# The output projections of both layers in weight units of 512 columns by 4 blocks, summed four token tiles at a time

## The chip, the cores and the metric

One core of a Trainium2 chip runs the whole program. The metric is the device time of one execution in microseconds (us), as the median of several runs. The engines are called by the profile's names: PE multiplies (PEld is its weight load), DVE is the vector engine, ACT the scalar engine, POOL the general one, SP issues most DMAs. Each engine takes its own instructions strictly in the order that was fixed when the program was built, and semaphores tie the engines together.

## What is computed

One inference step of a two-layer decoder. Layer 0 is a gated linear attention, layer 1 a differential attention; each ends with an output projection, and each is followed by a normalization and an MLP.

```python
def gla_output(o, r, g_norm, w_out, dtype):       # layer 0
    ...
    return o.astype(dtype) @ w_out
def diff_output(o, g_sub, lam_init, w_out, dtype):  # layer 1
    ...
    return o.reshape(B, T, DIFF_HEADS * DIFF_DV).astype(dtype) @ w_out
def post_norm(x, f, g, b):
    return layer_norm(DEEPNORM_ALPHA * x + f, g, b)
```

The 1024 prompt tokens are multiplied in each layer by a weight `w_out` of 1024 x 1024 in fp32. The result is added to the residual (times ALPHA) and normalized; the MLP of that layer reads the normalized rows. Beside this, eight running sequences are attended over 256 pages of keys and 256 pages of values in a cache; that work is spread as background over layer 0's projection, its MLP and layer 1's input projection.

## The kernel before

**The projection.** `w_out(w, scaled, side)` (L1004 to L1030) is called twice: for layer 0 at L1154 (`scaled` False) and for layer 1 at L1492 (`scaled` True). It multiplies 8 tiles of 128 tokens with the weight, whose 1024 rows are 8 blocks k of 128. An fp32 product is made of three matmuls (`mm3`, L205 to L208): the activations are held as a high part XH and a rest XL, the weight as whi and wlo, and XH x whi, XH x wlo and XL x whi are summed in one psum bank. The activations (128 x 128) are the operand that is loaded into PE, the weight's columns stream past.

The weight comes in *units* of 2048 columns in SBUF, each a pair whi, wlo. A unit here (`kunit`, L198) is all 8 blocks by 256 columns. `unit` (L182 to L196) loads it in four chunks of 128 x 512: for each a DMA from SP into a buffer `raw` (two of them, in pool wrp), a cast on ACT to whi (L193), a subtraction on POOL to wlo (L194). A chunk of a `kunit` covers two blocks by 256 columns, in rows of 1 KB.

The pool wsp holds two whi and two wlo, so two units are on chip at a time; the next unit takes the buffer of whichever unit is let go first, and its first cast waits for the last matmul that reads the old one.

**The order.** The four units u are taken with the two token halves c (tiles 0 to 3, tiles 4 to 7) as (0,0) (1,0) (0,1) (1,1) (2,0) (3,0) (2,1) (3,1): (u, c). For each pair there are two accumulations; each fills one psum bank `mmt` with two token tiles of 256 columns (24 matmuls for a tile, 48 for a bank). There are three mmt banks, three axt banks (for transposes, and for some of the MLP's tiles in layer 1) and two smt banks. A full bank is added to the residual Y by one DVE instruction of 128 x 512 (L1022 in layer 1; L1024 in layer 0, with ALPHA). After every odd u the two tiles are handed to `normalize` (L1040), which takes their statistics per 512 columns (L1045), and after the second 512 columns normalizes pairs of tiles (L1049 to L1060); after tile 3 and after tile 7 `to_fm` (L1066) transposes the four tiles through axt banks and makes XH and XL, or in layer 1 XR, for the MLP.

**What sets the order of instructions.** The program is written in the order above, and a planner turns it into the order of each engine when it is built: of what is ready by its own estimate of times, the earliest written goes first. So PE may take matmuls of a later tile while an earlier one waits, as far as psum banks and weights allow. Background work (`background`, L852: the pages) has the lowest priority.

**Around layer 0.** Before it PE ends the gate projection, whose last unit lets its buffer go shortly before `w_out` starts. At the same time SP issues four loads of the residual (1 MB each, L1151) and begins with pages of keys (512 KB each, L880), each multiplied by the query on DVE or POOL (L911) and reduced on DVE (L912). `side` is the generator of pages; `w_out` calls it 12 times. Some pages are tied behind the last step in `steps_v`, the list of DVE steps that the evictions (L1024) are added to. Behind it comes `mlp` (L1097), whose first two units follow in the wsp buffers.

**Around layer 1.** The planner starts `w_out` while the last head of the attention still runs: `o_fm` (L1339) turns the attention's output of one block k and one token half into XH and XL: four transposes on PE (L1343), ACT (L1344), DVE (L1345). Token half 0 is made early, half 1 only after the last head (block by block, k from 0 to 7), so matmuls of half 0 fill PE's gaps in between. The psum pools are opened anew here: the mmt banks lie where the attention's score banks (`prt`) were. The residual comes back from DRAM (L1442). `side` is one step there, the small tokens' normalization. Behind it comes `mlp1` (L1672), whose tiles take axt and mmt in turn, and whose DVE work (L1700, L1560, L203) begins before `w_out` ends.

Of the kernel before, what the change touches and what calls it, by code (L numbers as in the profile page):

```python
# [16 lines left out]
ALU = mybir.AluOpType  # L17
# [4 lines left out]
P = 128  # L22
D = 1024
T = 1024
NB = 8
# [6 lines left out]
ALPHA = 4.0 ** 0.25  # L32
# [82 lines left out]
def hybrid_step(ctx, tc, A, dbg=None, upto=9):  # L115
    nc = tc.nc
    V, S, G, TE = nc.vector, nc.scalar, nc.gpsimd, nc.tensor
# [21 lines left out]
    def pairt():  # L139
        return banks["pr"].tile([P, 2, 512], F32, name="prt")  # L140

    def mmt():
        return banks["mm"].tile([P, 512], F32, name="mmt") if "mm" in banks else pairt()[:, 0]

    def axt():
        return banks["ax"].tile([P, 512], F32, name="axt")
# [22 lines left out]
    def xh_part(c, i):  # L169
        return cp.tile([P, 4, TH], F32R, name="XH%d%d" % (c, i), tag="XH%d%d" % (c, i))  # L170

    XH = Halves([[xh_part(c, i) for i in range(2)] for c in range(2)])
    XL = Halves([cp.tile([P, NB, TH], F32R, name="XL%d" % c, tag="XL%d" % c) for c in range(2)])
    Y = cp.tile([P, 8192], F32, name="Y")
    Yt = Y.rearrange("p (t n) -> p t n", n=D)
# [6 lines left out]
    def unit(n, *srcs):  # L182

        hi = wsp.tile([P, 2048], F32R, name="whi")
        lo = wsp.tile([P, 2048], F32R, name="wlo")
        at = 0
        for src in srcs:
            step = 512 // n
            for x in range(0, src.shape[1], step):
                raw = wrp.tile([P, 512], F32, name="raw")  # L190
                dma(raw.rearrange("p (k n) -> p k n", n=n), src[:, x : x + step, :])
                c = slice(at, at + 512)
                S.copy(hi[:, c], raw)  # L193
                G.tensor_tensor(lo[:, c], raw, hi[:, c].bitcast(F32), op=ALU.subtract)  # L194
                at += 512
        return hi, lo  # L196

    def kunit(w, c0):  # L198
        return unit(256, w.rearrange("(k p) n -> p k n", p=P)[:, :, c0 : c0 + 256])
# [5 lines left out]
    def mm3(ps, ah, al, bh, bl, first, last):  # L205
        TE.matmul(ps, ah, bh, start=first, stop=False)  # L206
        TE.matmul(ps, ah, bl, start=False, stop=False)  # L207
        return TE.matmul(ps, al, bh, start=False, stop=last)  # L208
# [121 lines left out]
    hv, lv = (w.rearrange("p (i k n) -> p i k n", i=2, n=P) for w in qku)  # L330
# [12 lines left out]
    ps = smt()  # L343
# [16 lines left out]
    ps = smt()  # L360
# [156 lines left out]
    parts = []  # L517
# [9 lines left out]
    for k in range(NB):  # L527
        w = sload(wi[k * P : (k + 1) * P, 0:2048])
# [6 lines left out]
    for k in range(0, NB, 2):  # L535
        w = sload2(wi[:, 2048:3072], k)
# [20 lines left out]
    ps = smt()  # L557
# [4 lines left out]
    ps = smt()  # L562
# [3 lines left out]
    pv = ps.rearrange("p (h c t) -> p c h t", h=GH, c=4)  # L566
# [4 lines left out]
    ps = smt()  # L571
# [15 lines left out]
    ps = smt()  # L587
# [5 lines left out]
    for hh in range(2):  # L593
        ps = smt()
# [13 lines left out]
    ps = smt()  # L608
    pv = ps[:TS, :128].rearrange("p (h t) -> p h t", t=TS)
# [3 lines left out]
    for s in (8, 4, 2, 1):  # L613
        u = t2()[:, :128]
        level(sb.rearrange("p h t -> p (h t)"), sqk[:, :128], sqk[:, 128:], u, s, V)
        ps = smt()
        pv = ps[:TS, :128].rearrange("p (h t) -> p h t", t=TS)
# [53 lines left out]
    ps = smt()  # L671
# [125 lines left out]
    for h in range(1, GH):  # L797
# [6 lines left out]
        for c in range(2):  # L804
            parts = decays(h, c, pgs[c])
# [7 lines left out]
    for h in range(GH):  # L813
        hi, lo = kunit(wi, 2048 + h * 256)
        hv, lv = (w.rearrange("p (k n) -> p k n", n=256) for w in (hi, lo))
        silt = st2.rearrange("p k (c n) -> p k c n", c=2)
        for c in range(2):
            cs = slice(512 * c, 512 * c + 512)
            sil, pts = [], []
            for m in range(2):  # L820
                ps = mmt()
# [43 lines left out]
    lv = lpt[:, :256].rearrange("p (i j d) -> p i j d", i=2, j=2)  # L865
# [137 lines left out]

    def w_out(w, scaled, side=None):  # L1004

        units = {}
        n = 0
        for u, c in ((0, 0), (1, 0), (0, 1), (1, 1), (2, 0), (3, 0), (2, 1), (3, 1)):
            if u not in units:
                units[u] = kunit(w, u * 256)  # L1010
            hv, lv = (x.rearrange("p (k n) -> p k n", n=256) for x in units[u])
            for i2 in range(2):
                ps = mmt()
                t0 = 4 * c + 2 * i2
                for i in range(2):
                    a = slice((t0 + i) * P, (t0 + i + 1) * P)
                    for k in range(NB):
                        mm3(ps[:, i * 256 : (i + 1) * 256], XH[:, k, a], XL[:, k, a], hv[:, k, :], lv[:, k, :], k == 0, k == NB - 1)
                yv = Yt[:, t0 : t0 + 2, u * 256 : (u + 1) * 256]
                pv = ps.rearrange("p (i n) -> p i n", n=256)  # L1020
                if scaled:
                    V.tensor_tensor(yv, yv, pv, op=ALU.add)  # L1022
                else:
                    steps_v.append(V.scalar_tensor_tensor(yv, yv, ALPHA, pv, ALU.mult, ALU.add).ins)  # L1024
                if side and (n == 4 if scaled else n < 12):
                    next(side)
                n += 1
                if u % 2:
                    for t in (t0, t0 + 1):
                        yield t, u // 2  # L1030

    def ln_stats(pool):
        st = pool.tile([P, 8, 2, 6], F32, name="bst")
# [4 lines left out]
    steps_v, steps_g = [], []  # L1038
# [162 lines left out]
    units, outs = {}, []  # L1201
    for u, t2_ in ((u, t) for u in range(12) for t in range(4)):
# [5 lines left out]
        hv, lv = units[u]  # L1208
        ps = mmt()
        for i in range(2):  # L1210
            t = 2 * t2_ + i
            a = slice(t * P, (t + 1) * P)
# [6 lines left out]
        if u < 8:  # L1219
            tmp = qt.tile([P, 2, 4, 16], F32, name="qr")  # L1220
            pv = ps.rearrange("p (i n d) -> p i n d", i=2, d=64)
# [129 lines left out]
    ps = smt()  # L1351
# [36 lines left out]
    for step in steps + [None] * 0:  # L1388
        if step:
            h, n, t = step  # L1390
# [19 lines left out]
        if n % 4 == 3:  # L1410
            ts = (slice(0, 4), slice(4, 8))[n // 4] if h == 7 else slice(t % 2, 8, 2)
            S.copy(Yd[:, ts, h], po.rearrange("p (t e) -> p t e", e=P))
            for i in range(4):
                x = po[:, i * P : (i + 1) * P]
# [85 lines left out]
    acc = [smt(), smt()]  # L1500
# [246 lines left out]
```

## Time and profile before

| | us |
|---|---|
| median of 3 runs | 2808.88 (2805.65 to 2810.58) |
| the profiled execution | 2803.96 |
| its span, first to last instruction | 2802.2 |
| mean granted clock of PE | 0.993 |
| layer 0's `w_out`, its first matmul to the first of the MLP | 489.0 to 582.9 |
| layer 1's `w_out`, its first matmul to its last | 2000.3 to 2112.9 |
| evictions L1022 and L1024 | 16 each, 0.69 each |

The span is what the profile shows; the execution's own time has 1.8 us more around it. Matmul rows show a duration that overlaps the next one's, so the price of a matmul is the distance between starts, not the duration. In rows of groups, "idle before" is the idle time of that engine just before the group's instructions, with what ended it.

### The profile page before, as it was taken

To read this page: it belongs to the slowest core of one execution; us is meant where nothing else is said; L and a number is where in the kernel's file an instruction comes from. 1 tells how busy PE (TensorE), PEld (TensorE's weight loads), DVE (VectorE), ACT (ScalarE), POOL (GpSimd) and SP (SyncE) were. 2 spreads that over 40 slices of the span, in tenths; PEclk is the share of its full clock that TensorE was granted. 3 is DMA by queue.
4 is the path that set the end of the run, shared out by engine and by line. 5 is a ranking of instruction groups with operands and counts; after the bars stand their busy time and mean duration, and the time that the engine had idled before them with its cause. 6 is when DMAs were issued, how large, how long until landed. Compare 5 with 4: busy or idle time off the path is not lost.

```text
span 2802.2 us, 52241 instructions
## 1 busy us (share of the span) xinstructions
PE 2715.8 (97%) x19849; PEld 2233.8 (80%) x19849; DVE 1954.0 (70%) x3045; ACT 1096.4 (39%) x2233; POOL 1105.1 (39%) x744
## 2 busy tenths in 40 slices
PE   8988999999999999999999999999999999999997
PEld 5866767987777777777798988776899889797985
DVE  5466463668877777777677730887648888979788
ACT  4324363152231221221241112777535546355553
POOL 2142112243443343433234222100026677687774
PEclk9999999999999999999999999999999999999998
DMA  7565654735889898888658995122144455555584
GB/s 234 168 231 194 215 183 170 267 96 183 311 317 335 307 351 307 315 319 305 235 197 302 363 365 169 55 61 74 37 120 91 102 146 115 141 121 122 132 187 91
DMA packets 275624, 562.81 MB, mean 201 GB/s; under 512 B 23510, under 2 KB 144412, under 8 KB 271276
## 3 DMA queue, kind: packets, MB, share of 16 engines
q1 hardware_dynamic: 256076, 522.75, 54.1%
q0 software_dynamic: 19296, 36.71, 8.1%
q8 instruction: 156, 2.56, 0.4%
q14 instruction: 96, 0.79, 0.1%
HBM read 533.00 MB, written 29.52 MB: 201 GB/s over the span
## 4 chain that ended last, share of the span: by engine, by line
PE 74%; DVE 8%; ACT 4%; DMA 3%; issue 2%; POOL 1%; SPq 0%; DVEq 0%; POOLq 0%; ACTq 0%
PE mmt L206 17%; PE mmt L207 17%; PE mmt L208 17%; PE smt L952 4%; PE axt L206 3%; PE axt L207 3%; PE axt L208 3%; PE smt L1323 2%; ACT as L1301 2%; DVE pg L911 1%; PE prt L1297 1%; DMA swt<-in_mlp_w 1%; PE axt L1318 1%; DMA rw<-in_mlp_w 1%; PE smt L686 1%
## 5 line engine op out<-in xcount | busy, mean ns | idle before, releaser
L194 POOL TENSOR_TENSOR wlo<-raw,whi 128x512 fp32r<-128x512 f32 x252 | 364.4, 1459 | 730.6 <-ACT whi L193 599.6
L206 PE MATMUL mmt<-whi,XH 128*128 128x256 f32 (+1 forms) x1760 | 524.6, 300 | 1.3 <-DVE ast L1299 0.9
L207 PE MATMUL mmt<-wlo,XH 128*128 128x256 f32 (+1 forms) x1760 | 522.2, 298 | 0.4 <-POOL wlo L194 0.4
L206 PE MATMUL mmt<-XH,whi 128*128 128x512 f32 (+1 forms) x1216 | 434.2, 358 | 6.6 <-DVE Y L1022 3.0
L208 PE MATMUL mmt<-XH,wlo 128*128 128x512 f32 (+1 forms) x1216 | 432.0, 356 | 0.0
L208 PE MATMUL mmt<-whi,XL 128*128 128x256 f32 x1536 | 431.7, 284 | 0.0
L193 ACT CAST whi<-raw 128x512 fp32r<-128x512 f32 x252 | 150.5, 620 | 579.3 <-PE mmt L208 189.6
L206 PEld LDWEIGHTS mmt<-whi,XH 128*128 128x128 f32 x1760 | 330.7, 189 | 39.1 <-issue 24.3
L912 DVE TENSOR_REDUCE sc<-pg 128x16 f32<-128x1024 f32 x256 | 308.2, 1211 | 70.5 <-POOL pg L911 68.1
L207 PEld LDWEIGHTS mmt<-wlo,XH 128*128 128x128 f32 x1760 | 332.2, 189 | 17.5 <-issue 6.8
L207 PE MATMUL mmt<-XL,whi 128*128 128x512 f32 x768 | 306.9, 400 | 0.0
L911 DVE TENSOR_TENSOR pg<-pg,qb 128x1024 f32<-128x1024 f32 x192 | 262.7, 1375 | 57.9 <-DMA pg<-in_cache_k 46.8
L208 PEld LDWEIGHTS mmt<-whi,XL 128*128 128x128 f32 x1536 | 288.3, 189 | 4.4 <-issue 3.8
L206 PEld LDWEIGHTS mmt<-XH,whi 128*128 128x128 f32 x1216 | 229.0, 189 | 50.8 <-issue 7.5
L911 POOL TENSOR_TENSOR pg<-pg,qb 128x1024 f32<-128x1024 f32 x64 | 165.4, 2585 | 253.1 <-DMA pg<-in_cache_k 168.4
L208 PEld LDWEIGHTS mmt<-XH,wlo 128*128 128x128 f32 x1216 | 229.4, 189 | 36.4 <-issue 3.7
L206 PE MATMUL mmt<-whi,HH 128*128 128x512 f32 x512 | 204.6, 401 | 4.9 <-DVE Y L1136 3.4
L208 PE MATMUL mmt<-whi,HL 128*128 128x512 f32 x512 | 203.9, 398 | 0.0
L207 PE MATMUL mmt<-wlo,HH 128*128 128x512 f32 x512 | 203.4, 397 | 0.0
L1586 POOL TENSOR_TENSOR wlo<-RW,whi 128x512 fp32r<-128x512 f32 x96 | 166.1, 1767 | 58.1 <-ACT whi L1585 58.0
L1586 POOL TENSOR_TENSOR wlo<-rw,whi 128x512 fp32r<-128x512 f32 x92 | 156.8, 1778 | 79.1 <-ACT whi L1585 78.8
L207 PEld LDWEIGHTS mmt<-XL,whi 128*128 128x128 f32 x768 | 145.2, 189 | 38.4 <-issue 7.2
(438 smaller groups left out, 5707.8 us busy)
## 6 DMA issues: line engine op xcount, KB each, us to landing
pg<-in_cache_k SPq DMA_DIRECT2D x256, 512.0 KB
pg<-in_cache_v SPq DMA_DIRECT2D x256, 512.0 KB
raw<-in_mlp_w SPq DMA_DIRECT2D x164, 256.0 KB
swt<-in_mlp_w SPq DMA_DIRECT2D x32, 1024.0 KB
rw<-in_mlp_w SPq DMA_DIRECT2D x116, 256.0 KB
RW<-in_mlp_w POOLq DMA_DIRECT2D x96, 256.0 KB, 5.8
swt<-in_gla_w_in SPq DMA_DIRECT2D x12, 1024.0 KB
swt<-in_diff_w_in SPq DMA_DIRECT2D x12, 1024.0 KB
```

What stands on the lines that cost most here:

```text
L193: S.copy(hi[:, c], raw)
L194: G.tensor_tensor(lo[:, c], raw, hi[:, c].bitcast(F32), op=ALU.subtract)
L206: TE.matmul(ps, ah, bh, start=first, stop=False)
L207: TE.matmul(ps, ah, bl, start=False, stop=False)
L208: return TE.matmul(ps, al, bh, start=False, stop=last)
L686: TE.matmul(ps[o : o + TS, :], lhs[:, k + 2 * j + i, :], ts[j][:, i, c * 512 : (c + 1) * 512], start=k == 0 and j == 1, stop=k == nk - 4 a ...
L911: eng.tensor_tensor(pg, pg, qb, op=ALU.mult)
L912: return V.tensor_reduce(sc[:, n, :], pg.rearrange("p (h d) -> p h d", d=64), op=ALU.add, axis=AX.X).ins
L952: m = TE.matmul(acc[i * TS : i * TS + 16, :256], w[r, n, :], pg[r, i * 256 : (i + 1) * 256], start=n == 0, stop=n == NPG).ins
L1301: S.activation(sc_[:, m, :W], sc_[:, m, :W], AF.Exp, bias=mns[:, m : m + 1], scale=-1.0, accum_out=l[:, m : m + 1])
L1323: TE.matmul(out, at, v, start=j == 0, stop=j == t + 1)
L1586: G.tensor_tensor(lo[:, k, :], t, hi[:, k, :].bitcast(F32), op=ALU.subtract)
```

## The change

Both calls of `w_out` get another tiling. A unit is now 4 blocks by 512 columns (as in the MLP's second weight, L1129), so the two units of one half u of the columns are its upper and lower 512 rows (kk = 0, 1). Both are asked for at the top of u. For each token half c four accumulations are open at once, one tile of 512 columns each, in three mmt banks and one axt bank. They are first summed over unit kk = c (4 tiles x 4 blocks x 3 matmuls), then over unit 1 - c, and each tile is evicted when its second pass ends: the same 16 evictions of 128 x 512 in each layer. A matmul streams 512 columns instead of 256, so there are 384 in a layer instead of 768. A DMA row is 2 KB instead of 1 KB, a chunk is one block by 512 columns. Half c = 1 begins with unit 1 and ends with unit 0. The pages are called 12 times still, now at every second half of a tile (odd n below 24), before the eviction instead of behind it; layer 1's `side` step comes at n = 9 of 32 instead of n = 4 of 16.

```diff
-        units = {}
         n = 0
-        for u, c in ((0, 0), (1, 0), (0, 1), (1, 1), (2, 0), (3, 0), (2, 1), (3, 1)):
-            if u not in units:
-                units[u] = kunit(w, u * 256)
-            hv, lv = (x.rearrange("p (k n) -> p k n", n=256) for x in units[u])
-            for i2 in range(2):
-                ps = mmt()
-                t0 = 4 * c + 2 * i2
-                for i in range(2):
-                    a = slice((t0 + i) * P, (t0 + i + 1) * P)
-                    for k in range(NB):
-                        mm3(ps[:, i * 256 : (i + 1) * 256], XH[:, k, a], XL[:, k, a], hv[:, k, :], lv[:, k, :], k == 0, k == NB - 1)
...
-                if side and (n == 4 if scaled else n < 12):
-                    next(side)
-                n += 1
-                if u % 2:
-                    for t in (t0, t0 + 1):
-                        yield t, u // 2
+        for u in range(2):
+            parts = [w[512 * kk : 512 * kk + 512, 512 * u : 512 * u + 512].rearrange("(k p) n -> p k n", p=P) for kk in range(2)]
+            halves = [[x.rearrange("p (k n) -> p k n", n=512) for x in unit(512, part)] for part in parts]
+            for c in range(2):
+                acc = [mmt(), mmt(), mmt(), axt()]
+                for kk in (c, 1 - c):
+                    hv, lv = halves[kk]
+                    for i, ps in enumerate(acc):
+                        t = 4 * c + i
+                        a = slice(t * P, (t + 1) * P)
+                        for k in range(4):
+                            x = 4 * kk + k
+                            mm3(ps, XH[:, x, a], XL[:, x, a], hv[:, k, :], lv[:, k, :], kk == c and k == 0, kk != c and k == 3)
+                        if side and (n == 9 if scaled else n % 2 and n < 24):
+                            next(side)
+                        n += 1
+                        if kk == c:
+                            continue
+                        yv = Yt[:, t, 512 * u : 512 * u + 512]
...
+                        yield t, u
```

More of the change, by code (lines that the diff above doesn't have):

```diff
@@ L1004, in w_out @@
     def w_out(w, scaled, side=None):
-        units = {}
         n = 0
-        for u, c in ((0, 0), (1, 0), (0, 1), (1, 1), (2, 0), (3, 0), (2, 1), (3, 1)):
-            if u not in units:
-                units[u] = kunit(w, u * 256)
-            hv, lv = (x.rearrange("p (k n) -> p k n", n=256) for x in units[u])
-            for i2 in range(2):
-                ps = mmt()
-                t0 = 4 * c + 2 * i2
-                for i in range(2):
-                    a = slice((t0 + i) * P, (t0 + i + 1) * P)
-                    for k in range(NB):
-                        mm3(ps[:, i * 256 : (i + 1) * 256], XH[:, k, a], XL[:, k, a], hv[:, k, :], lv[:, k, :], k == 0, k == NB - 1)
[L1019 to L1024, printed above, removed]
-                if side and (n == 4 if scaled else n < 12):
-                    next(side)
-                n += 1
-                if u % 2:
-                    for t in (t0, t0 + 1):
-                        yield t, u // 2
@@ new lines, in w_out @@
+        for u in range(2):
[17 more added lines that the diff above has]
+                        yv = Yt[:, t, 512 * u : 512 * u + 512]
+                        if scaled:
+                            V.tensor_tensor(yv, yv, ps, op=ALU.add)
+                        else:
+                            steps_v.append(V.scalar_tensor_tensor(yv, yv, ALPHA, ps, ALU.mult, ALU.add).ins)
+                        yield t, u
```

## The prediction

> **What bounds the kernel now.** I read the page first: who is busy, and what the chain that ended last consists of.
>
> ```profile
> span 2802.2 us, 52241 instructions
> PE 2715.8 (97%) x19849; PEld 2233.8 (80%) x19849; DVE 1954.0 (70%) x3045; ACT 1096.4 (39%) x2233; POOL 1105.1 (39%) x744
> PE 74%; DVE 8%; ACT 4%; DMA 3%; issue 2%; POOL 1%; SPq 0%; DVEq 0%; POOLq 0%; ACTq 0%
> ```
>
> PE is busy for 97% of the span and is 74% of the chain: a microsecond saved on PE is a microsecond saved at the end, unless something else is late next. So I looked at PE in the two stretches that the change touches, first as busy time by stretch (length, then PE, PEld, DVE, ACT, POOL busy and instructions, granted clock, DMA share, GB/s), then as the list of its waits: around layer 0's stretch one row, around layer 1's the other five.
>
> ```profile
> 489.00:582.90 93.90, 93.90 (x799) 93.90 (x796) 54.35 (x88) 22.88 (x35) 27.76 (x20) 1.00 0.65 218
> 2000.30:2112.90 112.60, 111.71 (x951) 111.09 (x952) 55.27 (x96) 37.91 (x73) 26.22 (x20) 1.00 0.36 104
> PE mmt L206 <- DVE HL L203: 1.5, 1, 1.5
> ...
> PE mmt L206 <- DVE Y L1022: 3.0, 1, 3.0
> PE mmt L206 <- DVE ast L1299: 0.9, 2, 0.6
> ...
> PE axt L1071 <- ACT XR L1077: 0.4, 1, 0.4
> PE mmt L206 <- ACT XH L1344: 0.2, 1, 0.2
> ```
>
> In layer 0 PE does not stop once in 93.9 us, at clock 1.00: 768 matmuls of 256 columns and 32 transposes lie back to back. Its one wait of 1.5 us comes later, in the MLP. In layer 1 it loses 0.9 us inside the stretch and 3.0 us just behind it. All that better ordering could return is therefore 6.0 us (1.5 + 3.0 + 0.9 + 0.4 + 0.2), and only the three last rows and the 3.0 us lie near the projection. The rest of any gain has to come from cheaper matmuls. In a kernel of 2808.88 us, 0.2% is 5.6 us, about what a measurement can tell from no change.
>
> **The change part by part. 1. The matmuls.** 768 matmuls of 256 columns in each layer become 384 of 512, over both layers 768 pairs that each become one. Their price is the distance between starts. I take an undisturbed stretch of layer 1's projection, and one of layer 0's second MLP weight, which already has the new form (4 blocks by 512 columns, weights streaming). L206 is every third matmul.
>
> ```profile
> L206 PE MATMUL mmt<-whi,XH x58: 277/280/283, 2065.7 to 2085.9; 128*128 128x256 f32 x58
> L206 PE MATMUL mmt<-whi,HH x27: 392/397/400, 640.4 to 658.7; 128*128 128x512 f32 x27
> ```
>
> 20.2 us over 57 x 3 steps are 118.1 ns; 18.3 us over 26 x 3 are 234.6 ns. A pair costs 236.2, so merging saves 1.6 ns, and 768 x 1.6 = 1.3 us. The starts are rounded to 0.1 us, which leaves 2.5 ns of doubt in a pair: from 3.2 us gained to 0.6 lost. I take -1.3: the granted clock is 1.00 in both.
>
> The Trainium skill, page "TensorE: Matmul & The Clock Gate", section on why a gap is 56 ns and not 53.3, gives a warm matmul N columns at 2.4 GHz plus a fixed 2.5 ns or so. By that rule each merging would save the whole fixed part, 768 x 2.5 = 1.9 us, and the sum would come out 0.6 us lower. Here the two rows disagree with it in kind: they lie 11 and 21 ns above N / 2.4, so most of the excess grows with the columns and is not saved; the measured 1.6 ns decides.
>
> **2. Evictions and loads.** The 16 evictions of 128 x 512 stay (0.68 us each, first row), and so do the chunks of 256 KB with a cast and a subtraction each. They cost nothing as long as a unit is there when PE wants it. In the rows before, a unit is let go at 523.38 and at 538.87 (ACT's first cast follows at once) and complete when POOL's last row ends, at 533.41 and 547.30:
>
> ```profile
> L1024 DVE SCALAR_TENSOR_TENSOR Y<-Y,mmt 128x512 f32<-128x512 f32 x15 | 10.3, 684 | 23.0 <-PE mmt L208 22.9
> 523.38 1.14 ACT L193 CAST whi<-raw 128x512 fp32r<-128x512 f32 x2 [14.89 <-PE mmt L208]
> 538.87 1.23 ACT L193 CAST whi<-raw 128x512 fp32r<-128x512 f32 x2 [6.82 <-DMA raw<-in_gla_w_out]
> 530.52 2.89 POOL L194 TENSOR_TENSOR wlo<-raw,whi 128x512 fp32r<-128x512 f32 x2 [2.88 <-ACT whi L193]
> 546.01 1.29 POOL L194 TENSOR_TENSOR wlo<-raw,whi 128x512 fp32r<-128x512 f32 x1 [0.25 <-ACT whi L193]
> ```
>
> That is 10.0 and 8.4 us. In the new order half c = 1 reads unit 1 first and unit 0 last; unit 1 is let go one pass early, and a pass over one unit is 4 x 4 x 3 = 48 matmuls x 234.6 ns = 11.3 us. So the next half's first unit has 11.3 us for 10.0, and the second, let go at the turn, again 11.3 for 8.4. Cost 0, covered by that pass, with 1.3 us to spare at the tighter place; a load slower by more than that would show as a stall of the difference.
>
> **3. Layer 0's second unit.** This is the place with the least cover. The unit's last chunk is issued late, behind loads of the residual, and lands late:
>
> ```profile
> 499.09 2.46 SPq L191 DMA_DIRECT2D raw<-in_gla_w_out  x2
> 507.87 0.62 ACT L193 CAST whi<-raw 128x512 fp32r<-128x512 f32 x1 [13.06 <-DMA raw<-in_gla_w_out]
> 508.57 1.29 POOL L194 TENSOR_TENSOR wlo<-raw,whi 128x512 fp32r<-128x512 f32 x1 [14.96 <-ACT whi L193]
> 509.67 0.51 PE L206 MATMUL mmt<-whi,XH 128*128 128x256 f32 x3
> ```
>
> Its whi is ready at 508.49, its wlo at 509.86. Before, PE had 22 us of work on the first unit alone (both token halves), and the last row, three L206 in a row for three open banks, shows it arriving just then without a stop. Now only 11.3 us are on the first unit, and half 1 starts with the late one. But three of its four blocks are there by then: 36 matmuls x 234.6 = 8.4 us. 489.0 + 11.3 + 8.4 = 508.7, and the 8 matmuls that need only the last block's whi last 1.9 us more, to 510.6. If PE goes block by block through its four open banks, nothing is lost; if it goes tile by tile, it stops at 502.4 (three blocks, 9 matmuls, after 500.3) until 509.9, which is 7.5 us. The planner already ordered around this chunk once, so I take nearly the lower end, +0.4, for the banks, which now fill nearly together and wait for DVE behind its pages; ends 0 and 7.5.
>
> **4. Layer 1's start.** PE stops twice while XH, XL and banks arrive.
>
> ```profile
> 2000.30 0.36 PE L206 MATMUL mmt<-whi,XH 128*128 128x256 f32 x1 [0.22 <-DVE ast L1299]
> ...
> 2001.09 0.39 PE L206 MATMUL mmt<-whi,XH 128*128 128x256 f32 x1 [0.19 <-ACT XH L1344]
> ...
> 2002.23 0.39 PE L206 MATMUL mmt<-whi,XH 128*128 128x256 f32 x1 [0.64 <-DVE ast L1299]
> ```
>
> A matmul twice as long fills more of the same gap, but the bank that PE waits for at 2002.23 (a score bank that DVE still reads) comes no sooner. Of 0.8 us (0.19 + 0.64) I take half: -0.4; ends 0 and -0.8.
>
> **5. Layer 1's token half 1.** Until the last head is done PE lives on half 0:
>
> ```profile
> 2000.30:2033.30 33.00, 21.81 (x155) 19.20 (x156) 2.06 (x3) 0.00 (x0) 1.00 0.22 69
> 2033.93 1.61 DVE L1345 SCALAR_TENSOR_TENSOR XL<-axt,gs,XH 128x512 fp32r<-128x512 f32 x2 [3.17 <-ACT XH L1344]
> 2043.06 0.75 DVE L1345 SCALAR_TENSOR_TENSOR XL<-axt,gs,XH 128x512 fp32r<-128x512 f32 x1
> ```
>
> By 2033.30 it had used 156 of the 192 matmuls that units 0 and 1 have for half 0, 18.4 us. The new half 0 holds as much, 96 x 234.6 = 22.5 us, so 4.1 us are left, and the 32 transposes of half 1 go between (0.1 us each: what 768 x 118.1 ns = 90.7 us leaves of layer 0's 93.9 us, over its 32): PE is fed until 2033.3 + 4.1 + 3.2 = 2040.6. Before, half 1 started with block 0, one of the two of the 2033.93 row; now it starts with block 4, which the last row shows ready at 2043.81. Taken as it stands, PE stops for 3.2 us. But DVE made two blocks in 1.61 us when it had them, so with PE free for the transposes block 4 could come at 2033.9 + 5 x 0.8 = 2037.9, before the gap. I take +0.8, nearer to the second, since PE's own filler is what held the blocks up; ends 0 and 3.2.
>
> **6. Layer 1's end.** The 3.0 us wait is for a psum bank:
>
> ```profile
> 2103.36 6.21 DVE L1700 SCALAR_TENSOR_TENSOR Y<-Y,RP 128x1024 f32<-128x1024 f32 x3 [0.48 <-PE axt L1071]
> 2111.72 0.68 DVE L1022 TENSOR_TENSOR Y<-Y,mmt 128x512 f32<-128x512 f32 x1
> 2118.18 0.67 DVE L1022 TENSOR_TENSOR Y<-Y,mmt 128x512 f32<-128x512 f32 x1
> 2118.91 0.39 PE L206 MATMUL mmt<-XH,whi 128*128 128x258 f32 x1 [3.01 <-DVE Y L1022]
> ```
>
> PE ended the projection at 2112.9, but DVE, busy with the MLP's own preparation (L1700 and others), evicted the last mmt bank only at 2118.18; the MLP's third mmt tile waited for it. In the new order the last tile sits in an axt bank; the three mmt banks are summed up one tile (12 matmuls, 2.8 us), two and three tiles before the end. DVE's jam stays, but the bank that PE wants next is asked for at least 2.8 us earlier, about the length of the wait. I take -2.5; ends 0 (DVE evicts late again) and -3.0. What is late next is the normalization of the last tiles (the 0.4 us wait for XR), which hangs on the axt bank's eviction as before: 0.
>
> **7. Statistics and side calls.** Tile 6 is now ready 2.8 us before tile 7, so one L1045 (a 128 x 512 pass like an eviction's, about 0.7 us) leaves the chain behind the last eviction. In layer 0 PE then has the MLP's half 0 to do, 96 matmuls or 22.5 us, so this is worth 0 there. The pages' calls keep their number; the first two are no longer tied behind an eviction, so a page that lands late can hold DVE's queue, the evictions behind it and thus the banks; this is in part 3's +0.4.
>
> **Sum.** -1.3 + 0.4 - 0.4 + 0.8 - 2.5 = -3.0 us. The profiled execution took 2803.96 us (span 2802.2 and 1.8 around it), 4.9 us under the median of the three runs; it would become 2801.0. The median of 2808.88 becomes 2805.9.
>
> **The rivals. All of the idle time goes (faster).** Every PE wait quoted above disappears and the matmuls save their 1.3 us: 6.0 + 1.3 = 7.3 us, 2801.6. For it: all waits are at places that the change re-orders, and the 1.5 us of layer 0's MLP hang on DVE, whose chain there starts with the normalization that gets tile 6 sooner. Against it: that one is behind pages, and PE's first stops in layer 1 come from the attention.
>
> **The second unit is late (slower).** PE's order in layer 0 comes out tile by tile, and PE stands from 502.4 to 509.9: +7.5 us. An order that strict also finds nothing to fill the other gaps with, so only the matmuls' 1.3 us stand against it: +6.2, 2815.1. For it: half of the cover is gone, and all matmul banks but two axt are taken. Against it: three blocks are there in time, and the planner ordered around the same chunk before. It decides at the last chunk's landing: it costs nothing until 508.7, and everything behind that.
>
> **Only the matmuls change.** The other stops stay or are replaced by equal ones: -1.3, 2807.6. For it: 97% of PE busy leaves little, and waits tend to move.
>
> **How the numbers follow.** Forecast 0.46, all idle gone 0.27, late unit 0.15, only the matmuls 0.12. The predicted time is the forecast's, 2805.9. Its own bounds are within 0.2% of before except a tenth of its chance (0.05), where the ends of parts 1, 4 and 6 add up. So faster is 0.27 + 0.05 = 0.32, same 0.41 + 0.12 = 0.53, slower 0.15. The range reaches from the fast rival with half of the runs' spread (2.5 us) below it, 2799, to the slow one, 2815: what lies outside is about half of each of these two, 0.2.
>
> **What would show it.** Right: 384 matmuls of 128x512 with XH in each stretch, 234.6 ns apart; no PE wait between 500 and 512, with L206 in a run of four open banks there; no wait for L1022 of 3 us behind layer 1's projection; first casts of the next units while PE is still on the other one. Wrong in part 3: PE waiting for whi L193 or wlo L194 near 502. Wrong in part 5: PE idle near 2041 until XL L1345. Wrong in part 2: a PE wait for whi or wlo at either turn of u. The whole is wrong if PE's busy time in the two stretches changes by more than 3 us, or if the time moves with these stretches' lengths unchanged, in the pages or the MLP.

## The result, and the profile after

The changed kernel takes 2821.67 us (median of 16 runs, 2811.61 to 2825.21); the kernel before, beside it, 2810.92 (16 runs, 2803.17 to 2821.24). The ratio is 1.0033, 95% interval 1.0023 to 1.0043: slower, by 6 to 12 us. 2805.9 and a range up to 2815 had been predicted.

The profile's page, in the changed kernel: the span, the engines' busy time, the shares of the chain that ended last.

```profile
span 2810.8 us, 50701 instructions
PE 2719.2 (97%) x19081; PEld 2197.9 (78%) x19081; DVE 1962.7 (70%) x3045; ACT 1096.9 (39%) x2233; POOL 1091.4 (39%) x744
PE 77%; DVE 9%; DMA 5%; ACT 4%; issue 3%; POOL 2%; SPq 0%; DVEq 0%; POOLq 0%; ACTq 0%
```

The span is 8.6 us longer, 768 matmuls are gone, and PE is still busy for 97%: on this level nothing shows. So I went by stretches. In the changed kernel, in order: layer 0's projection without its end; the whole of it; its end; layer 1's projection. Columns as before (length; busy time and instructions of PE, PEld, DVE, ACT, POOL; granted clock; DMA share; GB/s).

```profile
488.05:553.09 65.04, 65.04 (x285) 52.75 (x282) 37.21 (x51) 9.23 (x16) 19.80 (x13) 1.00 0.83 282
488.05:588.22 100.17, 96.25 (x421) 77.29 (x418) 59.14 (x92) 24.23 (x36) 23.71 (x18) 0.97 0.57 193
574.60:588.50 13.90, 11.40 (x47) 8.84 (x48) 7.55 (x13) 7.58 (x12) 2.13 (x2) 0.75 0.00 1
2006.48:2119.63 113.15, 110.87 (x566) 91.42 (x567) 54.10 (x102) 36.50 (x72) 19.98 (x19) 1.00 0.31 95
```

Up to 553 PE never stops, over the late second unit too. Layer 0's stretch is 6.3 us longer (93.90 before), and the loss is at its end: in the last 14 us PE is idle for 2.5 and its clock is 0.75. Layer 1's stretch has about its old length (112.6 before). The waits of PE from 484 to 660 in the changed kernel (total, times, longest) name what it stands for; before, the 1.5 us for DVE HL was the only one:

```profile
PE axt L1071 <- DVE XL L203: 3.4, 3, 1.5
PE mmt L206 <- DVE HL L203: 2.7, 1, 2.7
PE mmt L208 <- POOL wlo L194: 2.4, 2, 2.1
```

And PE's timeline shows the place (start, length, what; in brackets the idle time before it and its releaser):

```profile
572.78 0.40 PE L208 MATMUL mmt<-whi,XL 128*128 128x512 f32 x1
574.65 0.63 PE L1071 MATMUL axt<-c_ident,Y 128*128 128x128 f32 x4 [1.47 <-DVE XL L203]
575.80 0.63 PE L1071 MATMUL axt<-c_ident,Y 128*128 128x128 f32 x4 [0.52 <-PE axt L1071]
577.86 2.21 PE L1071 MATMUL axt<-c_ident,Y 128*128 128x128 f32 x8 [1.43 <-DVE XL L203]
580.53 1.09 PE L1071 MATMUL axt<-c_ident,Y 128*128 128x128 f32 x4 [0.47 <-DVE XL L203]
581.29 0.77 PE L206 MATMUL axt<-whi,XH 128*128 128x512 f32 x1
581.85 0.63 PE L207 MATMUL axt<-wlo,XH 128*128 128x512 f32 x1
...
587.99 0.39 PE L208 MATMUL axt<-whi,XL 128*128 128x512 f32 x1
```

What the reader is to see: with the three mmt tiles of the last half done, PE transposes block after block of half 0, each waiting for a bank that DVE (XL) frees. Only behind the last block do the 24 matmuls of tile 7 come, both passes in one piece. Tile 7's sum lies in an axt bank. `to_fm(0)` asks for its eight axt banks when tile 3 is handed on, which in the program's text is ahead of the place where half c = 1 asks for its own; with three banks, tile 7 came last. Its first pass reads unit 1, so that buffer goes free late, and the MLP's first weights come late with it (POOL wlo, above): ACT begins to cast them when that pass is done, at 585.62, where it was 569.75 before.

```profile
585.62 1.14 ACT L193 CAST whi<-raw 128x512 fp32r<-128x512 f32 x2 [2.52 <-PE axt L208]
```

Along the program: the changed kernel begins the projection 0.9 us early, has its first MLP down eviction (L1136) 7.9 us late and its end 8.6 us late. So most of the loss is made between those first two marks. Layer 1's first projection matmul comes 6.2 us late, and the first down eviction of layer 1's MLP (L1659) 4.7: there 1.5 us are gained. The last 3.9 us are lost behind that mark, where the change edits nothing: from there to the end it is 592.5 us before, 596.4 in the changed kernel, and 592.1 with the new projection in layer 1 alone (below), so they do not follow from the new order in layer 1.

### The profile page after: what moved, and what is told of

Same layout as the page of the kernel before. It is cut to its first block, busy times and chain, and to the rows that moved or that the text cites. A ratio compares the mean times of both kernels' runs of the same rounds, so it can differ in the third digit from the quotient of the medians.

```text
span 2810.8 us, 50701 instructions
## 1 busy us (share of the span) xinstructions
PE 2719.2 (97%) x19081; PEld 2197.9 (78%) x19081; DVE 1962.7 (70%) x3045; ACT 1096.9 (39%) x2233; POOL 1091.4 (39%) x744
## 4 chain that ended last, share of the span: by engine, by line
PE 77%; DVE 9%; DMA 5%; ACT 4%; issue 3%; POOL 2%; SPq 0%; DVEq 0%; POOLq 0%; ACTq 0%
PE mmt L206 18%; PE mmt L207 17%; PE mmt L208 17%; PE smt L952 4%; PE axt L206 4%; PE axt L207 4%; PE axt L208 4%; PE smt L1323 2%; ACT as L1301 1%; DMA swt<-in_mlp_w 1%; DVE pg L911 1%; PE prt L1297 1%; DVE XH L203 1%; DVE Y L1659 1%; PE axt L1318 1%
## 5 line engine op out<-in xcount | busy, mean ns | idle before, releaser
L194 POOL TENSOR_TENSOR wlo<-raw,whi 128x512 fp32r<-128x512 f32 x252 | 358.2, 1434 | 741.2 <-ACT whi L193 605.0
L206 PE MATMUL mmt<-whi,XH 128*128 128x256 f32 (+1 forms) x1440 | 456.1, 319 | 0.9 <-DVE ast L1299 0.6
L207 PE MATMUL mmt<-wlo,XH 128*128 128x256 f32 (+1 forms) x1440 | 454.7, 316 | 0.4 <-POOL wlo L194 0.4
L208 PE MATMUL mmt<-whi,XL 128*128 128x256 f32 (+1 forms) x1216 | 363.7, 302 | 0.0
L912 DVE TENSOR_REDUCE sc<-pg 128x16 f32<-128x1024 f32 x256 | 308.1, 1211 | 57.4 <-POOL pg L911 54.9
L206 PEld LDWEIGHTS mmt<-whi,XH 128*128 128x128 f32 x1440 | 270.2, 188 | 47.4 <-issue 26.4
L207 PEld LDWEIGHTS mmt<-wlo,XH 128*128 128x128 f32 x1440 | 271.4, 189 | 26.5 <-issue 7.6
L208 PEld LDWEIGHTS mmt<-whi,XL 128*128 128x128 f32 x1216 | 228.7, 189 | 11.1 <-issue 3.0
```

Of the source, the lines that this page charges most:

```text
L912: return V.tensor_reduce(sc[:, n, :], pg.rearrange("p (h d) -> p h d", d=64), op=ALU.add, axis=AX.X).ins
```

## The experiments

The stretch from layer 0's first projection matmul to the first L1136 is called the *front* below: 149.8 us before (489.00 to 638.77), 158.6 after (488.05 to 646.66). A ratio is against runs of the kernel before on the same chip (medians 2806.56 to 2812.59 in the five groups); fronts are of the one profiled execution. The same front, profiled in two kernels, came out as 149.8 and 150.7 (the kernel before, and the new projection in layer 1 alone) and as 158.6 and 157.9 (changed, and layer 0 alone), so a difference of 1 us between fronts says nothing. Theory A was that the axt bank is the cause, with the half clock and the late unit that follow from it; rival B that any new order costs some microseconds in many places.

**Which layer.** The old `w_out` was kept beside the new one and called for the other layer.

```diff
-normalize(w_out(A["diff_w_out"][0], True, samples()), ...      # layer0_only
+normalize(w_out_old(A["diff_w_out"][0], True, samples()), ...
-normalize(w_out(A["gla_w_out"][0], False, paged), ...          # layer1_only
+normalize(w_out_old(A["gla_w_out"][0], False, paged), ...
```

> The new projection in layer 0 alone; layer 1 keeps the old one. Theory A (tile 7's axt bank in layer 0 is claimed first by the eight transposed blocks of half 0; PE stands 6.6 us, runs at half clock behind that, and the second weight unit is freed late): nearly the whole loss, 8 to 10 us over the kernel before, ratio 1.003, with the stretch from the first projection matmul to the last near 100 us and PE waiting there for DVE XL. Rival B (the loss is spread: other waits and lower clock in the stretches behind, which any new order brings): about half of it, 4 to 5 us, and the other half in layer 1.

> The new projection in layer 1 alone. Theory A: nothing is lost, 0 to 3 us faster than the kernel before (1.3 us of matmuls and the 3.0 us wait behind the stage, against some new idle at its start). Rival B: 4 to 5 us slower.

Layer 0 alone: 2822.54 us, ratio 1.0052 (1.0033 to 1.0072), front 157.9; 16 us between medians, where 8 to 10 had been expected. Layer 1 alone: 2807.35, ratio 1.0000 (0.9986 to 1.0014). The loss is all layer 0's; rival B's even split falls.

**The fourth bank.** Two edits that let tile 7 go ahead of the transposes: another bank, or the same bank with the tiles of half 0 handed on later. Both act in layer 1 too, where they were not followed.

```diff
-acc = [mmt(), mmt(), mmt(), axt()]          # fourth_in_smt
+acc = [mmt(), mmt(), mmt(), smt()]
```
```diff
-yield t, u                                   # pages_late
+held.append((t, u))
+if (u, c) == (1, 0):
+    continue
+yield from held
+held.clear()
```

> As the changed kernel, but the fourth sum of each group lies in an smt bank, which nobody else asks for there. Theory A: tile 7's matmuls no longer come behind the transposes, layer 0's stretch is 93 to 95 us long, no stop of PE for DVE XL and no half clock in it, the MLP's first casts begin near 570 instead of 585.6; the time is 0 to 3 us under the kernel before, ratio 0.999 to 1.000. Rival B: the stop goes or moves, but the time stays 4 us or more over the kernel before, ratio 1.0015 to 1.003, in waits and dips of the clock further on.

> As the changed kernel with its axt bank, but the last column half hands its first four tiles to the normalization only together with tile 4, so that tile 7 asks for its bank ahead of the transposes. Theory A: as with the smt bank, layer 0's stretch 93 to 95 us and no stop for DVE XL; half 0 is normalized some 10 us later, which may cost up to 3 us at the MLP's start; the time is within 3 us of the kernel before. A rival of A (it is the number of banks, not who asks first): the stop of 6 us or more stays, since the axt banks are three as before. Rival B: 4 us or more over the kernel before.

With the smt bank ("the smt kernel" from here on) the stop is gone: PE is busy for all of the projection, at clock 1.00.

```profile
490.65:583.33 92.68, 92.68 (x417) 75.31 (x413) 54.92 (x87) 21.04 (x31) 27.50 (x20) 1.00 0.63 220
```

With the late handing-on, too, tile 7 comes ahead of most transposes, in its axt bank: who asks first decides, not the number of banks. So theory A has its cause right. But the times do not follow: 2815.04, ratio 1.0023 (1.0010 to 1.0036), front 157.6 for the smt kernel; 2818.15, ratio 1.0042 (1.0026 to 1.0057), front 163.2 for the other. In the smt kernel the stop was repaired, and others came in its place, in the MLP's first group: three waits of PE for DVE HL, 7.5 us in all, where the kernel before has one of 1.5. In the other kernel PE waits 7.6 us up to 660, for HL, XH, XL and wlo; how much of that its late handing-on costs was not separated. The longest stop of the smt kernel, in PE, ACT, DVE and POOL:

```profile
606.83 0.70 PE L206 MATMUL mmt<-XH,whi 128*128 128x512 f32 x1 [4.03 <-DVE HL L203]
601.96 1.12 ACT L202 CAST HH<-mmt 128x512 fp32r<-128x512 f32 x2
604.96 1.22 DVE L912 TENSOR_REDUCE sc<-pg 128x16 f32<-128x1024 f32 x1 [2.88 <-POOL pg L911]
606.10 1.28 DVE L203 TENSOR_TENSOR HL<-mmt,HH 128x512 fp32r<-128x512 f32 x2
602.59 2.34 POOL L911 TENSOR_TENSOR pg<-pg,qb 128x1024 f32<-128x1024 f32 x1 [5.56 <-DMA pg<-in_cache_k]
```

Read backwards: PE wants an mmt bank. DVE frees it with HL, whose input ACT has ready at 603.08; but HL stands in DVE's queue behind the reduction (L912) of a page. That waits for POOL's multiplication, and this for the page's DMA. (The Trainium skill, page "TensorE: Matmul & The Clock Gate", section "Architectural detail: the array is 16× 32×32, not 1× 128×128", calls DVE's queue a strict FIFO; the 3.02 us that HL lay ready agree.) The kernel before has the same late page at nearly the same time, but there both HL stand ahead of it (the second is shown), and PE never notices:

```profile
600.32 0.69 DVE L203 TENSOR_TENSOR HL<-mmt,HH 128x512 fp32r<-128x512 f32 x1 [0.19 <-ACT HH L202]
604.18 1.22 DVE L912 TENSOR_REDUCE sc<-pg 128x16 f32<-128x1024 f32 x1 [3.17 <-POOL pg L911]
```

This became theory D: with the new tiling the planner writes DVE's and POOL's queues anew, and background pages now stand ahead of what PE needs. In the smt kernel the four tiles of half 0 are evicted in one burst (554.26 to 561.40) with page work between them, ACT's first normalizations start at 564.9 (561.7 before), and HL slips behind the page.

**Without page calls in the projection**, in all three kernels; those pages are done later, so the three are compared with each other.

```diff
-normalize(w_out(A["gla_w_out"][0], False, paged), ...
+normalize(w_out(A["gla_w_out"][0], False), ...
```

> The kernel before, without the twelve page calls in layer 0's projection (those pages come later, in the calls at the end of the MLP's first group; nothing is left out). It is the base for the two kernels without page calls. Theory D (a late page at the head of DVE's or POOL's queue holds the evictions that PE waits for in the MLP's first group): PE's wait of 1.5 us for DVE HL near 639 goes; the pages now pile up later, so its time lies anywhere from 3 us under to 10 us over the kernel before.

> The changed kernel without those twelve page calls. Theories A and D together: the fourth sum's axt bank still costs its 6 to 8 us (the stop for DVE XL in layer 0 stays), the waits for DVE HL and POOL wlo in the MLP's first group go, so it is 4 to 8 us over the kernel before without page calls. Rival E (the pages have nothing to do with it; the new order of tiles makes half 1's normalization late): 9 us or more over it, with the same waits.

> The fourth sum in an smt bank and no page calls in layer 0's projection. Theories A and D: both causes are gone, and it is within 2 us of the kernel before without page calls, or up to 3 us under it; PE has no stop of over 1 us for DVE HL between 590 and 650. Rival E: 5 to 8 us over it, as with the page calls (6.5 us).

Measured: 2843.45 (ratio 1.0129, 1.0111 to 1.0148), 2847.32 (1.0144, 1.0126 to 1.0163) and 2826.86 (1.0062, 1.0048 to 1.0076). The heap of pages behind costs every one of them more than was expected, but the order has turned: the smt kernel is clearly faster than the kernel before under the same rule, by 16.6 us between medians, and the axt bank now costs 20.5. Not all of that is the projection's: the fronts differ by 2.3 and 8.7 us. Behind them, from 640 to 800, where the heap is worked off, PE waits 20.1 us in the kernel before and in the changed one, 16.2 in the smt kernel; where the rest is made was not followed. Up to 640 the smt kernel's only wait of PE is

```profile
PE mmt L208 <- POOL wlo L194: 0.8, 1, 0.8
```

Its ACT starts normalizing half 0 at 553.9; with pages it was 564.9. Rival E (late tiles, whatever the pages) falls, and by fronts theory D is borne out.

**The pages' calls elsewhere**, in the smt kernel: behind the first twelve evictions, or in the first twelve passes.

```diff
-if side and (n == 9 if scaled else n % 2 and n < 24):   # ahead of the eviction
+if side and (n == 4 if scaled else n < 12):             # smt_pages_after_evictions: behind it, n counts evictions
+if side and (n == 9 if scaled else n < 12):             # smt_pages_first
```

> The fourth sum in an smt bank, and the twelve page calls each behind one of the first twelve evictions (the kernel before has them behind the first twelve of sixteen pairs), none in a pass that only starts sums. Theory D: the pages' place decides, so the waits in the MLP's first group change: if they go, 0 to 3 us under the kernel before; if others come, up to 10 us over. Rival E: the 6.5 us stay, with PE waiting for DVE HL near 602 and 634.

> The fourth sum in an smt bank, and the twelve page calls in the first twelve passes, all in the first column half, so that no page is worked at between the evictions and statistics of the second. Theory D: half 0 is normalized early (ACT ends near 562), the waits for DVE HL near 602 go, and it is 1 to 4 us under the kernel before, a version that beats both. Theory F: the loads crowd the second column half's weights, PE waits for whi or wlo near 534 to 550, and it is over the kernel before. Rival E: 6.5 us over, as with the smt bank alone.

2816.54, ratio 1.0029 (1.0016 to 1.0041), front 157.8; and 2819.61, ratio 1.0028 (1.0013 to 1.0044), front 160.1. Other calls, another stop: the second has its own, of 6.3 us for DVE HL near 637. My idea that pages in the first column half would be out of the way failed. Loads did not crowd the weights either: PE waited for no whi or wlo, but 2.1 us for an eviction (L1029) at 541.

**Pages loaded, not computed**, in the kernel before and in the smt kernel.

```diff
 pg = page("cache_k", b, n)
+if b == 0 and n < 12:
+    return V.memset(sc[:, n, :], 0.0).ins
```

> The kernel before; the first twelve pages of the first sample are loaded as ever, but their multiplication and reduction are left out (a small memset stands for them), so the scores of those pages are not computed. It is the base for the next kernel. Theory D (pages hold the queues of DVE and POOL): 1 to 5 us under the kernel before, PE's 1.5 us for DVE HL near 639 may stay, since later pages are computed. If instead the pages' loads are what hurts (theory F: they take the DMA engines from the weights), no difference from the kernel before beyond 2 us.

> The fourth sum in an smt bank, the same twelve pages loaded and not computed. Theory D: half 0 is normalized 5 us earlier than with the pages' work (ACT's four passes end near 561 to 564 and not 569.6) and the stop of PE at 602 goes; it is 0 to 4 us under the kernel before with its pages unused, where it was 6.5 us over with pages computed in both. Theory F: the stop at 602 stays and it is 5 us or more over.

2821.14 (ratio 1.0041, 1.0027 to 1.0055) and 2814.31 (1.0018, 1.0004 to 1.0032); fronts 159.7 and 155.2. I had expected the kernel before to gain from having less to do; it became slower, and so the smt kernel, at 6.8 us under it, beats it by more than the 0 to 4 expected. DVE in the kernel before with pages unused (line numbers 2 higher: L1094 are the gain rows, L913 and L914 a page):

```profile
627.20 3.46 DVE L1094 SCALAR_TENSOR_TENSOR Y<-Y,ht 128x1024 f32<-128x1024 f32 x2 [1.93 <-DMA ht<-in_ln_mix_g]
630.58 2.29 DVE L913 TENSOR_TENSOR pg<-pg,qb 128x1024 f32<-128x1024 f32 x1
632.90 1.22 DVE L914 TENSOR_REDUCE sc<-pg 128x16 f32<-128x1024 f32 x1
634.04 2.35 DVE L1094 SCALAR_TENSOR_TENSOR Y<-Y,ht 128x1024 f32<-128x1024 f32 x2
636.30 1.88 DVE L203 TENSOR_TENSOR HL<-mmt,HH 128x512 fp32r<-128x512 f32 x3
```
```profile
PE mmt L206 <- DVE HL L203: 6.0, 1, 6.0
```

With less work DVE's queue was written in another order, three HL at once behind two rounds of gain rows and a page, and PE stood for 6.0 us. Less work and the same loads of pages made this kernel slower, so it is not the amount of work that costs; the rows point to the queue's order.

**The late pages taken off.** Every fourth page is multiplied by POOL and is tied to the statistics instead of the evictions, so those can be done in the MLP's first half. With all pages of the first sample on DVE none stands there.

```diff
-eng, after = (G, steps_g) if n % 4 == 3 else (V, steps_v)
+eng, after = (G, steps_g) if n % 4 == 3 and b else (V, steps_v)
```

> The kernel before, with the first sample's pages all multiplied on DVE (one in four went to POOL, tied to the statistics and not to the evictions, and all those behind it could run in the MLP's first group). Its written order of DVE then has no page work between the projection's evictions and the MLP's first down eviction; the pages come later. It is the base for the next three. Theory D: its 1.5 us wait for DVE HL may go or stay (the gain rows are still there), and some later pages come in a heap; 2 us under to 6 us over the kernel before.

> The changed kernel, with the first sample's pages multiplied on DVE. Theories A and D: what is left is the axt bank, 5 to 9 us over the kernel before with the same edit, with the stop of PE for DVE XL in layer 0 and half clock behind it. Rival E (the order of tiles makes the normalization late, pages or not): 9 us or more over it.

> The fourth sum in an smt bank, and the first sample's pages multiplied on DVE. Theory D: the stop near 602 goes, and by the first down eviction it is 1 to 4 us ahead of the kernel before with the same edit; its time is from 4 us under to 1 us over that kernel. Rival E: 5 us or more over it. If the gain rows with their one buffer are the holder, a stop of 3 to 6 us for DVE HL near 630 stays in both kernels.

2829.46 (ratio 1.0062, 1.0046 to 1.0078), 2829.96 (1.0061, 1.0043 to 1.0080), 2820.97 (1.0038, 1.0023 to 1.0052). Again the smt kernel is the fastest of its three, here by 8.5 us (3.5 in the front) with intervals that overlap a little, and again all pay for the pages later. The changed kernel is level with the kernel before, where 5 to 9 us over had been expected. The same with the gain rows in eight pieces of 128 columns through two buffers (`for j in range(8)`, HTB = 2):

> As the kernel with the fourth sum in an smt bank and the first sample's pages on DVE, and the gain rows loaded in eight pieces of 128 columns through two buffers (four pieces of 256 through one before), so that a row's load runs beside the work on the one ahead. If the gain rows are the holder: the waits of DVE for the rows' DMA go from about 2 us each to under 1, the stop of PE for DVE HL near 630 shrinks by 2 to 5 us, and the time by as much. If they are not: within 1 us of the kernel without this edit, or over it by the cost of twice as many instructions, some 2 us.

2826.08, ratio 1.0048 (1.0032 to 1.0064), 5 us over the one without, with intervals that overlap. DVE's waits for the rows were 0.33 to 1.92 us (1.73 to 3.05 in the one without), but thirteen of the sixteen passes now stood ahead of the last HLs, and PE waited 3.4 us where it had waited 1.9. Shorter waits for the rows did not shorten the stop, so the single buffer is not the holder; that the place in the queue is fits the rows, but no run moved it alone.

**Trying for a version that beats both.** Late pages (from the twelfth on) on DVE, with more calls ahead of the MLP or as many as before.

```diff
-eng, after = (G, steps_g) if n % 4 == 3 else (V, steps_v)
+eng, after = (G, steps_g) if n % 4 == 3 and (b or n < 12) else (V, steps_v)
-n % 2 and n < 24        # smt_late_pages_dve leaves this as it is
+n % 4 < 3 and n < 24    # smt_18_pages
+n < 16                  # before_16_pages (n < 12 before)
```

> The fourth sum in an smt bank; eighteen page calls in layer 0's projection (three of four passes up to the 24th), and the first sample's pages from the twelfth on multiplied on DVE. So 17 pages are done ahead of the MLP, none stands in DVE's queue among the MLP's first evictions, and no heap comes behind. Theory D: the first down eviction comes 2 to 5 us earlier than before, and the time is 0 to 5 us under the kernel before. If the loads of the pages crowd the weights: PE waits for whi or wlo in the projection and it is over the kernel before by 3 us or more.

> The kernel before with page calls behind all sixteen evictions of pairs, and the first sample's pages from the twelfth on multiplied on DVE: the old projection with the same rule for its pages. If the place of the pages is all that counts, as much faster as smt_18_pages (0 to 5 us under the kernel before); if the new projection has a gain of its own, 2 to 3 us over smt_18_pages.

> The fourth sum in an smt bank, the twelve page calls as in the changed kernel, and the first sample's pages from the twelfth on multiplied on DVE. Theory D: the stop near 602 goes, the first down eviction comes 2 to 4 us earlier than before; but pages are put off behind it as in smt_no_late_pages, so the time lies 2 to 8 us over the kernel before.

2820.03 (1.0041, 1.0026 to 1.0055), 2823.29 (1.0057, 1.0040 to 1.0074), 2815.65 (1.0025, 1.0011 to 1.0039); fronts 160.4, 160.1, 145.1. With eighteen calls DVE reduces 21 pages within the projection (11 in the kernel before and in the smt kernel), and PE waits for XH and XL of half 0, 3.4 and 3.0 us. The old order with sixteen calls is no better. The last has the second shortest front of all, and gives it back at the end of the MLP's first group, where DVE works off the pages that were put off:

```profile
686.91 7.95 DVE L911 TENSOR_TENSOR pg<-pg,qb 128x1024 f32<-128x1024 f32 x5
694.79 1.21 DVE L912 TENSOR_REDUCE sc<-pg 128x16 f32<-128x1024 f32 x1
...
702.71 0.67 DVE L203 TENSOR_TENSOR HL<-mmt,HH 128x512 fp32r<-128x512 f32 x1
```
```profile
PE mmt L206 <- DVE HL L203: 5.9, 1, 5.9
```

None of the versions beats the kernel before. All fronts under one rule each, with the pages reduced in them (the count of L912):

| pages | reduced in front | old `w_out` | new, axt | new, smt |
|---|---|---|---|---|
| as given | 19 | 149.8 | 158.6 | 157.6 |
| no calls in the projection | 3 | 147.3 | 153.7 | 145.0 |
| all on DVE | 11 | 149.8 | 151.5 | 146.3 |
| twelve not computed | 7 | 159.7 | | 155.2 |

With the smt bank the new tiling has the shorter front in three of four rules, by 2.3 to 4.5 us; over the axt bank, the smt bank is worth 8.7 and 5.2 us there, and 1.0 with the pages as given. Only in the rule that the kernel before was written with is it longer: there the old order gets 19 pages through with one stop of 1.5 us.

## Why the prediction was wrong

**The step that failed** is the price of the fourth accumulation's bank. The sum's only term for it is part 3's +0.4, "for the banks, which now fill nearly together and wait for DVE behind its pages"; beside it stand part 2's "They cost nothing as long as a unit is there when PE wants it" and part 7's zero for layer 0. Of the axt banks I wrote only that two were left. I did not count who else asks for them: `to_fm(0)`, eight times, and earlier in the program's text. What the runs showed in its place: 3.9 us of idle PE up to 588 (100.17 less 96.25), half clock behind it, unit 1 let go late, and a front 8.8 us longer. Another bank or another order of asking undoes this stop.

**The other half of that term failed beside it.** Part 7 put a page that holds DVE's queue into the same +0.4. Without the axt stop, the queues around the pages still cost the smt kernel 7.8 us of front; without the page calls, the axt bank costs 6.4 (153.7 against 147.3). The two do not add: each gives the other cover (8.8 with both). None of the prediction's signs named the bank; its last one, that the time moves in the pages or the MLP with the stretches' lengths unchanged, is what the smt kernel shows. The fronts before, changed and with the smt bank (columns as before):

```profile
489.00:638.77 149.77, 148.45 (x1052) 137.97 (x1048) 96.62 (x137) 53.53 (x86) 55.27 (x36) 1.00 0.55 179
488.05:646.66 158.61, 149.62 (x657) 119.88 (x654) 100.82 (x136) 51.37 (x82) 53.34 (x35) 0.97 0.52 169
490.65:648.27 157.62, 150.26 (x668) 121.29 (x664) 101.34 (x138) 53.15 (x87) 56.51 (x37) 0.98 0.52 177
```

PE is idle for 1.3, 9.0 and 7.4 us of them. So idle time is 7.7 of the 8.8 us and 6.0 of the 7.8; the rest is busy time, longer at the lower clock although the matmuls are cheaper.

**1. Matmuls:** too small. Spacing before and after, from rows of the two kernels:

```profile
L206 PE MATMUL mmt<-whi,XH x217: 276/280/384, 489.0 to 565.7; 128*128 128x256 f32 x109
566.02 0.49 PE L1071 MATMUL axt<-c_ident,Y 128*128 128x128 f32 x3
```
```profile
L206 PE MATMUL mmt<-whi,XH x24: 392/396/400, 516.0 to 532.1; 128*128 128x512 f32 x24
516.01 0.40 PE L206 MATMUL mmt<-whi,XH 128*128 128x512 f32 x1
532.74 0.39 PE L206 MATMUL axt<-whi,XH 128*128 128x512 f32 x1
```

77.02 us for 217 x 3 matmuls are 118.3 ns each; 16.73 us for 24 x 3 are 232.4. A pair saves some 4 ns, 768 pairs about 3.2 us, where I had 1.3, and 3.2 as the end of the range. By the Trainium skill's fixed 2.5 ns a matmul (page "TensorE: Matmul & The Clock Gate", section "Wait — 56ns, not 53.3ns?") the estimate was 1.9; the measured saving is larger than either.

**2. The turns of u:** right up to 553, with no wait for whi or wlo; behind that unit 1 was let go late (above). **3. The second unit:** its place was right, with no stop near 502, and the rival of the slow side did not come there; its +0.4 was for the banks. **4. Layer 1's start:** right; PE's waits for DVE ast and ACT XH there went from 1.1 to 0.6 us, where -0.4 was forecast. **5. Half 1 from block 4:** +1.8 against +0.8, inside its ends, but the working missed the fourth tile here too. It counted 96 matmuls of half 0 to fill PE; only the 72 of the three mmt tiles ran before half 1's first at 2042.32, and those of the axt tile began at 2050.93. The stops are transposes that wait for a bank which XL frees, not matmuls that wait for block 4. **6. Layer 1's end:** right; the 3.0 us for the psum bank are gone, a new 1.3 us wait for the MLP's wlo takes part of it. The waits of PE around layer 1's projection, and the two matmuls, changed kernel:

```profile
PE axt L1343 <- DVE XL L1345: 2.0, 5, 0.7
PE mmt L208 <- POOL wlo L1586: 1.3, 2, 0.6
PE mmt L206 <- DVE ast L1299: 0.6, 2, 0.4
```
```profile
2042.32 0.48 PE L206 MATMUL mmt<-whi,XH 128*128 128x512 f32 x1
...
2050.93 0.40 PE L206 MATMUL axt<-whi,XH 128*128 128x512 f32 x1
```

The net there is the 1.5 us of the section on the result; the ratio of layer 1 alone (1.0000) can't tell it from nothing.

**What stays open:** which order of DVE's queue would carry 19 pages beside the new tiling without a stop. The runs changed the order only through the planner, by where calls stand in the text; an order written out by hand was not tried. Nor was it separated how much of the loss behind the stops is the clock's, or why the kernels without page calls differ by so much more than their fronts.

## What to carry to other kernels

When a change takes one more bank or buffer from a pool, list who else asks for it and in which order they stand in the program, not only how many there are. Where one stop is repaired and the time hardly moves, look for the next one just behind it: two late things cover each other. And where queues are written by a planner, any edit rewrites them; a tuned kernel may owe microseconds to an order that nobody asked for, so price a change with the background work taken out on both sides as well as with it.

## What the runs showed of the hardware

A stop of a few microseconds can cost more than its length. Behind the stop of 4.03 us shown above, PE's matmuls in the smt kernel come at half clock:

```profile
607.34 0.63 PE L207 MATMUL mmt<-XL,whi 128*128 128x512 f32 x1
...
609.89 0.62 PE L207 MATMUL mmt<-XL,whi 128*128 128x512 f32 x1
...
610.59 0.40 PE L206 MATMUL mmt<-XH,whi 128*128 128x512 f32 x1
610.83 0.40 PE L207 MATMUL mmt<-XL,whi 128*128 128x512 f32 x1
```

Six steps in 2.55 us are 425 ns, against 232.4; the eight steps of the dip lose about 1.5 us. But the length of a stop does not tell alone. Granted clock (0.57, 1.00) in the 4 us behind a wait of 1.91 us in the smt kernel, and behind one of 3.27 us in the smt kernel with pages unused (by the first figure, (1 - 0.57) x 4 x 2 = 3.4 us at half rate):

```profile
633.80:637.80 4.00, 3.96 (x10) 3.13 (x11) 1.90 (x2) 1.10 (x2) 3.81 (x3) 0.57 0.49 155
```
```profile
642.40:646.40 4.00, 4.00 (x17) 3.27 (x18) 3.16 (x5) 0.62 (x1) 1.91 (x2) 1.00 0.38 92
```

The Trainium skill (page "TensorE: Matmul & The Clock Gate", section "Part 1: The HAM clock gate") puts half rate down to an idle window of about 3.4 us that runs free of the kernel. The half rate and the dip's length of some 3.4 us agree with these rows; that it takes a whole idle window does not agree with a dip behind 1.91 us. Over the two profiled executions the mean clock is 0.993 and 0.990, but it differs from one execution of a kernel to the next (0.988 to 0.994 in the 32 of the kernel before that ran beside layer 0 alone). The means are 0.991 over these 32 and 0.989 over the 16 of the changed kernel, which of 2810 us is about 5 us, an estimate of half the loss; how much of it lies on the critical path the runs do not separate.
